# Moving the side work of an encoder layer's MLP rounds to other slots, and four more changes of order

## Chip, cores and metric

The kernel runs on one core of one Trainium2 chip. The metric is the device time of one execution in microseconds (us); lower is better. TensorE is PE here, VectorE DVE, ScalarE ACT, GpSimd POOL, and SP is the engine that issues most DMAs.

## What is computed

One layer of an encoder over 2048 positions of width 1024, all in float32:

```python
u = rmsnorm(h, g_pre_mix)
proj = u @ w_in                                  # q, k, v of group a and of group b
o_a = rmsnorm(windowed_gqa_sink(qa, ka, va, ...), g_out_a)
o_b = rmsnorm(dilated_mixture(qb, kb, vb, ...), g_out_b)   # three dilated patterns, mixed by their weights
h = h + rmsnorm(concat([o_a, o_b]) @ w_o, g_post_mix)
a = relu(rmsnorm(h, g_pre_mlp) @ w_up)           # 4096 wide
h = h + rmsnorm((a * a) @ w_down, g_post_mlp)
gate = sigmoid(h @ w_ple_gate + b_ple_gate)
h = h + rmsnorm(gate * (p @ w_ple_proj), g_post_ple)
```

## The kernel before

Every float32 product is made from three matmuls of a rounded high part and a low remainder (`mm3`: high by high, high by low, low by high). The split of an operand is a pair of operations: ACT copies the value to a rounded high part and DVE subtracts that from the value to give the low part. A matmul has 512 columns as a rule; transposes on PE have 128.

The stages follow one another on PE: input projections; attention of group a; attention of group b; the output projection by tiles of 128 rows (`c_tile`); the MLP; the gate. Up to the end of the MLP the engines' instructions stand in the order that the code issues them. A clock of ticks sets that order: `later(dt, fn)` puts a piece of work `dt` ticks ahead, `tick()` issues what is due. Each engine then works through its own list in order and waits where an operand is not there. Behind the MLP, a scheduler orders the gate stage.

**Group b** has four pairs of heads. `mix` is a generator that joins the three patterns of a pair; each `yield` ends one step, and other work (scores of the next pair, and a filler: `wo_first`, the first part of the output projection, or the ple products `fill2`) is issued between two steps. Its last part turns the weights into a high part `ch` (ACT, L853) and a low part `cl` (DVE, L855), and multiplies both with a selection matrix on PE (`cps`, L861), in 8 parts `rr` of four matmuls; DVE scales the outputs by them (L864) and POOL adds the patterns. The ple products take a buffer for each result (L941, a copy on ACT), which a DMA issued by ACT takes to memory (L942): the first 8 results use the pool `sgt` with 2 buffers, the others 8 slots of `big`. Behind the last pair's scores, a loop issues the last mixer and the filler, and after it `schedule_c` sets the loads (L974), splits (`c_split`, L979 and L980) and norms of the 16 tiles of the output projection.

**`c_tile`** normalises a tile, adds the residual, stores h, normalises again (`norm2`, L1094) and transposes the result by two `turn`s (L1100) into the operands of the MLP. The first products of the MLP's first round (`up`, L173 to L175) are issued beside the last tiles.

**The MLP** has 32 rounds: two halves of the positions by 16 chunks of 256 of its 4096 columns. A round computes its own down products (`down`, L1288) in a two-by-two scheme of seven products, and beside them the up products of the next round. There are 28 ticks, in each three down matmuls and three or four up matmuls: 84 and 96 per round. The last round has no up products. DVE adds the products to `accs` (L1297), but for one product of four parts, ACT copies to `dmp` (L1294) and POOL adds (L1295); POOL also forms the sums of operands (`tmp`, L1132), and DVE their low parts (L1127). Two kinds of foreign work are put in with `later`: a `split_job` prepares a slice of the gate's weight, and a `post_job` (rounds 17 to 24) finishes one tile of the first half's MLP output: load, two squares on ACT (L1207), `rstd` on POOL (L1212 to L1215), two `scale`s (L1219) and two `add`s (L1223) on DVE, a store.

**The gate** has 16 tiles (`d_item`): load of h (`h2`, L1451, three buffers) and of the ple product (`pl`), eight transposes (L146), 48 matmuls (L137 to L139) into `psm`, then the bias (L1474), sigmoid (L1475), product (L1476), norm (L124; L1482), residual (L1483) and the store to `out`. For the first eight tiles it carries along the second half's post work (`post`, L1336 squares, L1345, L1348).

Of the kernel before, what the change touches and what calls it, by code (L numbers as in the profile page):

```python
# [59 lines left out]
def layer(ctx, tc, a, out):  # L60
# [592 lines left out]
    with ExitStack() as st:  # L653
# [159 lines left out]
        def mix(pair, tms, dns):  # L813
# [38 lines left out]
            ch, cl = wr[:, 0], wr[:, 1]  # L852
            act.activation(ch, wt, AF.Copy)  # L853
            yield
            dve.tensor_sub(cl, wt, ch.bitcast(F32))  # L855
            order = range(8) if pair < 3 else (0, 1, 4, 5, 2, 3, 6, 7)
            for n, rr in enumerate(order):
# [14 lines left out]
                if n != 6 or pair == 3:  # L872
                    yield
# [28 lines left out]
        def ple():  # L902
# [26 lines left out]
            for t in range(16):  # L929
                ph_, pl_ = cur  # L930
                for hf in range(2):
# [6 lines left out]
                    if 2 * t + hf == 8:  # L938
                        big = bm.tile([128, 8, 512], F32, name="pst", tag="v1")
                    mx = big[:, (2 * t + hf) % 8] if t >= 4 else sg.tile([128, 512], F32, name="sgt", tag="sgt")  # L940
# [112 lines left out]
    def c_tile(n, t, box):  # L1053
# [3 lines left out]
        cs = [slice(0, 512), slice(512, 1024)]  # L1057

# [33 lines left out]
        def norm2():  # L1092
            box["vn"] = acc_tile(n % 3 if n < 15 else 5)
            dve.scalar_tensor_tensor(box["vn"], box["mx"], box["r2"], gm, op0=ALU.mult, op1=ALU.mult)  # L1094

        def turn(h):
# [4 lines left out]
            if tb < 2:  # L1101
# [9 lines left out]
                4: [norm1], 5: [add], 6: [keep], 7: [norm2], 8: [lambda: turn(0)], 9: [lambda: turn(1)]}, half  # L1111
# [81 lines left out]
    def post_job(t, at):  # L1193
# [179 lines left out]
    with ExitStack() as st:  # L1373
# [5 lines left out]
        stack.append(st.enter_context(ExitStack()))  # L1379
        tp, fd, ap_ = right("tp", 6), right("fd", 4), right("ap_", 3)  # L1380
        fus.append(right("fu2"))
# [12 lines left out]
        jobs = [[(i, k) for i in range(2) for k in range(8)] for _ in range(2)]  # L1394
        for n in range(32):
# [132 lines left out]
```

## Time and profile before

| | us |
|---|---|
| median of 3 runs (2816.85 to 2821.08) | 2817.31 |
| the profiled execution: its own time | 2813.91 |
| the profiled execution: span | 2812.1 |
| PE busy | 2719.5 (97%) |
| DVE busy | 1767.2 (63%) |
| ACT busy | 1273.4 (45%) |
| POOL busy | 931.5 (33%) |

The busy times are of one execution, and the span of its records is 1.8 us shorter than its own time. A matmul's busy time in the profile is modelled, and a busy PE isn't PE at its peak. PEclk is the mean granted clock of TensorE as a share of full speed: 1.00 is 2.4 GHz, 0.50 is 1.2 GHz.

### The profile page before, as it was taken

Reading aid. Unit: us, or ns where it says so; the run is one execution under the profiler, and the core shown is the slowest. Engines: PE = TensorE matmul, PEld = TensorE weight load, DVE = VectorE, ACT = ScalarE, POOL = GpSimd, SP = SyncE. Lnnn points to the kernel's source line nnn. Section 1 sums busy time; section 2 is a strip of 40 time slices with the busy share of each in tenths; the row PEclk is TensorE's granted clock in tenths of the full one; section 3 lists DMA queues with packets and bytes.
Section 4 is the critical chain, followed back from the end, with each engine's and each line's share of the span. In section 5 each row is a group of like instructions: output and inputs, shape, how many; then the busy total and the mean of one; then the engine's idle time right before and its main releaser. Section 6 shows DMA issues by size and latency. Waiting matters only on the chain.

```text
span 2812.1 us, 38924 instructions
## 1 busy us (share of the span) xinstructions
PE 2719.5 (97%) x13952; PEld 2123.9 (76%) x13952; DVE 1767.2 (63%) x3420; ACT 1273.4 (45%) x2940; POOL 931.5 (33%) x950
## 2 busy tenths in 40 slices
PE   7999999999999998999999999999999999999998
PEld 6878866666677676878888888888777778887787
DVE  4210244456666653777778778776788787776665
ACT  4321355566666553555434434445444444443332
POOL 3000033331322301444434434534525344344220
PEclk9999999999999999999999999999999999999999
DMA  5232352325543325872312212234232323224453
GB/s 177 86 116 83 97 157 72 108 78 141 139 93 120 86 97 173 271 237 75 99 63 65 82 60 68 86 134 160 96 106 97 102 90 105 79 72 157 168 192 104
DMA packets 247441, 322.82 MB, mean 115 GB/s; under 512 B 19856, under 2 KB 175504, under 8 KB 244848
## 3 DMA queue, kind: packets, MB, share of 16 engines
q1 hardware_dynamic: 220112, 280.16, 31.6%
q10 hardware_dynamic: 27136, 40.18, 4.0%
q8 instruction: 110, 1.80, 0.3%
q14 instruction: 83, 0.68, 0.1%
HBM read 225.59 MB, written 102.04 MB: 117 GB/s over the span
## 4 chain that ended last, share of the span: by engine, by line
PE 54%; DVE 4%; issue 2%; POOL 1%; ACT 1%; DMA 1%; ACTq 0%; DVEq 0%; POOLq 0%; SPq 0%
PE psd L1288 11%; PE psy L1288 9%; PE psu L174 8%; PE psu L175 8%; PE psu L173 8%; PE psm L137 3%; PE psm L138 3%; PE psm L139 3%; DVE y L1219 1%; PE psd L137 1%; PE psd L139 1%; PE psd L138 1%; DVE acc L1297 1%; POOL acc L1295 1%; DVE y L1223 1%
## 5 line engine op out<-in xcount | busy, mean ns | idle before, releaser
L1297 DVE TENSOR_TENSOR acc<-acc,psd 128x512 f32<-128x512 f32 x488 | 331.3, 685 | 179.5 <-PE psd L1288 174.6
L174 PE MATMUL psu<-vt,uph 128*128 128x512 f32 x1024 | 407.4, 398 | 0.0
L175 PE MATMUL psu<-vt,upl 128*128 128x512 f32 x1024 | 405.0, 395 | 0.0
L173 PE MATMUL psu<-vt,uph 128*128 128x512 f32 x1024 | 402.1, 393 | 0.0
L1132 POOL TENSOR_TENSOR tmp<-rl 128x512 f32<-128x512 f32 x64 | 83.4, 1303 | 691.4 <-ACT rl L1276 691.4
L174 PEld LDWEIGHTS psu<-vt,uph 128*128 128x128 f32 x1024 | 192.3, 188 | 47.9
L173 PEld LDWEIGHTS psu<-vt,uph 128*128 128x128 f32 x1024 | 192.6, 188 | 45.0
L768 ACT ACTIVATE e<-e,tm 128x256 f32<-128x256 f32 (+1 forms) x384 | 176.7, 461 | 107.9 <-DVE tm L765 105.8
L175 PEld LDWEIGHTS psu<-vt,upl 128*128 128x128 f32 x1024 | 192.2, 188 | 43.6
L1297 DVE TENSOR_TENSOR acc<-acc,psy 128x512 f32<-128x512 f32 x248 | 168.8, 684 | 79.2 <-PE psy L1288 72.5
L1275 ACT ACTIVATE rl<-psu 128x512 f32<-128x512 f32 x128 | 76.4, 597 | 305.8 <-PE psu L175 305.8
L1295 POOL TENSOR_TENSOR acc<-acc,dmp 128x512 f32<-128x512 f32 x128 | 192.1, 1512 | 50.5 <-DVE al L1127 31.5
L133 DVE SCALAR_TENSOR_TENSOR wc<-wraw,pre_mix_t,wc 128x128 fp32r<-128x128 f32 x176 | 58.2, 378 | 233.7 <-ACT wc L132 233.7
L1288 PE MATMUL psd<-dnh,al 128*128 128x512 f32 x512 | 203.2, 397 | 0.0
L1288 PE MATMUL psd<-dnh,ah 128*128 128x512 f32 x512 | 201.3, 393 | 0.0
L1288 PE MATMUL psd<-dnl,ah 128*128 128x512 f32 x512 | 201.2, 393 | 0.0
L765 DVE CUSTOM_DVE_ANT_0 e<-ps_s,b 128x256 f32<-128x256 f32 (+1 forms) x384 | 122.7, 375 | 101.9 <-PE ps_s L752 101.6
L173 PE MATMUL psm<-uhi,wc 128*128 128x512 f32 x448 | 181.8, 410 | 0.3 <-ACT uhi L128 0.3
L174 PE MATMUL psm<-ulo,wc 128*128 128x512 f32 x448 | 177.9, 397 | 0.0
L175 PE MATMUL psm<-uhi,wc 128*128 128x512 f32 x448 | 177.6, 396 | 0.0
L1288 PE MATMUL psy<-dnh,ah 128*128 128x512 f32 x384 | 154.2, 402 | 19.0 <-DVE acc L1297 15.0
L1288 PE MATMUL psy<-dnh,al 128*128 128x512 f32 x384 | 153.0, 398 | 0.0
(703 smaller groups left out, 6259.8 us busy)
## 6 DMA issues: line engine op xcount, KB each, us to landing
upraw<-in_w_up_dram SPq DMA_DIRECT2D x64, 512.0 KB, 4.7
dnraw<-in_w_down_dram SPq DMA_DIRECT2D x64, 512.0 KB, 5.2
xt<-in_x_dram SPq DMA_DIRECT2D x32, 512.0 KB, 4.2
h<-hd SPq DMA_DIRECT2D x32, 512.0 KB, 4.4
wraw<-in_w_in_dram SPq DMA_DIRECT2D x26, 512.0 KB, 4.0
qkd<-sgt ACTq DMA_DIRECT2D x52, 256.0 KB, 2.3
mad<-sgt ACTq DMA_DIRECT2D x32, 256.0 KB, 2.0
acc<-mad SPq DMA_DIRECT2D x16, 512.0 KB, 6.3
```

The lines of the kernel that those rows point to most:

```text
L137: pe.matmul(ps, lh(k), rh(k), start=k == 0, stop=False)
L138: pe.matmul(ps, lh(k), rl(k), start=False, stop=False)
L139: pe.matmul(ps, ll(k), rh(k), start=False, stop=k == n - 1)
L173: pe.matmul(ps, lh(k), rh(k), start=k == 0, stop=False)
L174: pe.matmul(ps, lh(k), rl(k), start=False, stop=False)
L175: pe.matmul(ps, ll(k), rh(k), start=False, stop=k == n - 1)
L765: dve.tensor_tensor_reduce(ej, box["ps"][hh][:, 256 * jj : 256 * jj + w], bs[hh] if p == 2 else bs[hh][:, var], scale=1.0, scalar=3.0e38, ...
L768: act.activation(ej, ej, AF.Exp, bias=tm, scale=-1.0, accum_out=box["dn"][p][:, i : i + 1])
L1132: pool.tensor_tensor(t, x, y, op=op)
L1288: pe.matmul(ps, l[:, js], r, start=start and m == 0, stop=m == 2, skip_group_check=True)
L1295: pool.tensor_tensor(t, t, d, op=ALU.add)
L1297: dve.tensor_add(t, t, ps)
```

## The change

Five things are changed, in the order of the code.

1. In `mix`, the high part, the low part and the first `cps` matmuls stand in three steps rather than one and a half, and the 8 parts of the other three pairs are bunched as 0, 1, 2 with 3, 4 with 5, 6 with 7.
2. The ple products use the slots of `big` from their fourth result on, not from the ninth; the loop at the end of group b takes two filler steps always, not three in its first three turns; `schedule_c` is called in its eleventh turn rather than behind it.
3. The two turns of the last two output tiles are issued 3 and 5 ticks later, beside the first round of the MLP, and their results have buffers of their own.
4. In rounds 17 to 24 the steps of `post_job` are spread from ticks 6 to 14 to ticks 8 to 24, and these rounds have no `split_job`; rounds 16 and 25 to 29 have three each.
5. The last round of the MLP gets up's place filled by the gate: the transposes of tiles 0, 1 and 2 and the 96 matmuls of tiles 0 and 1 (`gate_first`), whose h is loaded in round 30. In the gate stage these are left out.

The diff, without the changes to pools and their closing and without repeated arguments:

```diff
@@ mix, the mixer of one pair of heads (group b) @@
             ch, cl = wr[:, 0], wr[:, 1]
+            yield
             act.activation(ch, wt, AF.Copy)
             yield
             dve.tensor_sub(cl, wt, ch.bitcast(F32))
+            yield
             order = range(8) if pair < 3 else (0, 1, 4, 5, 2, 3, 6, 7)
...
-                if n != 6 or pair == 3:
+                if n not in (2, 4, 6) or pair == 3:
                     yield
@@ the ple products, fill2 @@
-                    if 2 * t + hf == 8:
+                    if 2 * t + hf == 3:
                         big = bm.tile([128, 8, 512], F32, name="pst", tag="v1")
-                    mx = big[:, (2 * t + hf) % 8] if t >= 4 else sg.tile([128, 512], F32, name="sgt", tag="sgt")
+                    mx = big[:, (2 * t + hf) % 8] if 2 * t + hf >= 3 else sg.tile([128, 512], F32, name="sgt", tag="sgt")
@@ the end of group b @@
         while mixers:
             advance()
-            for _ in range(3 if loops < 3 else 2):
+            for _ in range(2):
                 next(fill2, None)
+            if loops == 10:
+                schedule_c(4)
+                start = clock[0] + 4
             loops += 1
             tick()
-        schedule_c(4)
-        for _ in range(4):
+        while clock[0] < start:
             next(fill2, None)
             tick()
@@ c_tile, one tile of the output projection @@
+        late = {14: 3, 15: 5}.get(n, 0)
...
-            box["vn"] = acc_tile(n % 3 if n < 15 else 5)
+            box["vn"] = acc_tile(n % 3 if n < 14 else n - 10)
...
-                ... 7: [norm2], 8: [lambda: turn(0)], 9: [lambda: turn(1)]}, half
+                ... 7: [norm2], 8 + late: [lambda: turn(0)], 9 + late: [lambda: turn(1)]}, half
@@ post_job @@
-        for dt, fn in ((0, fetch), (6, lambda: squares(0)), (7, lambda: squares(1)), (8, rstd), (10, lambda: scale(0)),
-                       (11, lambda: scale(1)), (12, lambda: add(0)), (13, lambda: add(1)), (14, keep)):
-            later(at + dt, fn)
+        for dt, fn in ((0, fetch), (8, lambda: squares(0)), (9, lambda: squares(1)), (10, rstd), (15, lambda: scale(0)),
+                       (17, lambda: scale(1)), (20, lambda: add(0)), (23, lambda: add(1)), (24, keep)):
+            later(dt, fn)
@@ before the rounds (new) @@
+        def gate_load():
+            for t in range(3):
+                h = ru.tile([128, D], F32, name="h0", tag="upraw") if t == 2 else vr.tile([128, D], F32, name="h0", tag="vraw")
+                sp.dma_start(h, hd[128 * t : 128 * t + 128, :])
+                heads[t] = [h]
+
+        def gate_turn(t, g):
...
+            ps = psu.tile([128, 4, 128], F32, name="psu", tag="psu")
+            for k in range(4):
+                pe.transpose(ps[:, k, :], h[:, 512 * g + 128 * k : 512 * g + 128 * k + 128], ident)
+            ks = slice(4 * g, 4 * g + 4)
+            act.activation(hi[:, ks], ps, AF.Copy)
+            low = lambda: dve.tensor_sub(lo[:, ks], ps, hi[:, ks].bitcast(F32))
...
+        def gate_first():
+            for hf in range(2):
+                for t in range(2):
+                    _, hi, lo = heads[t]
+                    ps = psu.tile([128, 512], F32, name="psu", tag="psu")
+                    yield from mm3_pieces(ps, 8, ...)
+                    y = heads[t, hf] = ox.tile([128, 512], F32, name="y0", tag="rl")
+                    act.activation(y, ps, AF.Copy)
+                if hf == 0:
+                    gate_turn(2, 0)
+                    gate_turn(2, 1)
@@ the rounds @@
-                for at in ((0, 14) if n < 3 else (0,)):
+                for at in ((0, 10) if n < 3 else (0,)):
                     split_job(0, *jobs[0].pop(0), at)
-            if 17 <= n < 30:
-                if n < 25:
-                    post_job(n - 17, 0)
-                for at in ((16,) if n < 20 else (0, 14) if n >= 25 else (16,)):
-                    if jobs[1]:
-                        split_job(1, *jobs[1].pop(0), at)
+            if 17 <= n < 25:
+                post_job(n - 17)
+            for at in (0, 9, 17) if n == 16 or 25 <= n < 30 else ():
+                if jobs[1]:
+                    split_job(1, *jobs[1].pop(0), at)
...
+            if n == 30:
+                later(20, gate_load)
+            if n == 31:
+                u = gate_first()
             done = 0
             for m in range(28):
                 next(d)
-                while u and done < (m + 1) * 32 // 28:
+                if n == 31 and m < 4:
+                    gate_turn(m // 2, m % 2)
+                while u and done < ((m + 1) * 32 // 28 if n < 31 else (m - 3) * 32 // 24):
                     next(u)
                     done += 1
@@ d_item, one tile of the gate stage @@
             def s2():
+                if t < 3:
+                    box.update(hh=heads[t][1], hl=heads[t][2])
+                    return
...
-                    ps = psm.tile([128, 512], F32, name="psm", tag="psm")
-                    mm3(ps, 8, ...)
+                    if t < 2:
+                        ps = heads[t, hf]
+                    else:
+                        ps = psm.tile([128, 512], F32, name="psm", tag="psm")
+                        mm3(ps, 8, ...)
```

On PE, in the mixer of the first pair, the first `cps` matmuls, the filler (`psm`) and the next pair's scores (`ps_s`, `po`, `pt`) stood so before:

```order
L173 MATMUL psm<-wo,oh__6493 128x512
L174 MATMUL psm<-wo,oh__6493 128x512
L175 MATMUL psm<-wo,ol__6494 128x512
L752 MATMUL ps_s<-bk,bq 128x128 x4
L796 MATMUL po<-et,v_5797 64x128 x4
L779 MATMUL pt<-ident,e 128x128 x4
L861 MATMUL cps<-wr,sel 128x384 x4
L173 MATMUL psm<-wo,oh__6493 128x512
```

and now:

```order
L174 MATMUL psm<-wo,oh__6493 128x512
L175 MATMUL psm<-wo,ol__6494 128x512
L173 MATMUL psm<-wo,oh__6493 128x512
L174 MATMUL psm<-wo,oh__6493 128x512
L175 MATMUL psm<-wo,ol__6494 128x512
L752 MATMUL ps_s<-bk,bq 128x128 x4
L796 MATMUL po<-et,v_5797 64x128 x4
L779 MATMUL pt<-ident,e 128x128 x4
L863 MATMUL cps<-wr,sel 128x384 x4
L752 MATMUL ps_s<-bk,qn 128x256 x4
```

Before, a filler piece with `oh__6493` (six matmuls, of which the row shows the first) still followed the first four `cps`; now all of them stand ahead, and the first `cps` come two steps later, a step being one filler piece and one piece of scores. The line numbers of the changed kernel are 2 to 53 higher.

On DVE, in round 19 (`y` is post_job's tile, `acc` the running sums, `rstd` comes from POOL), the two scales and the first add stood so before:

```order
L1297 TENSOR_TENSOR acc_17773<-acc_17773,psd 128x512
L1127 TENSOR_TENSOR dnl<-tmp,dnh 128x512
L1297 TENSOR_TENSOR acc_17774<-acc_17774,psd 128x512
L1219 SCALAR_TENSOR_TENSOR y_18857<-y_18857,rstd,gb 128x512
L1297 TENSOR_TENSOR acc_17775<-acc_17775,psd 128x512
L1219 SCALAR_TENSOR_TENSOR y_18857<-y_18857,rstd,gb 128x512
L1127 TENSOR_TENSOR al<-tmp,ah 128x512
L1297 TENSOR_TENSOR acc_17776<-acc_17776,psy 128x512
L1223 TENSOR_TENSOR y_18857<-y_18857,h_18859 128x512
L1297 TENSOR_TENSOR acc_17777<-acc_17777,psy 128x512
L1223 TENSOR_TENSOR y_18857<-y_18857,h_18859 128x512
```

and now:

```order
L1302 TENSOR_TENSOR acc_17767<-acc_17767,psy 128x512
L1132 TENSOR_TENSOR al<-tmp,ah 128x512
L1302 TENSOR_TENSOR acc_17768<-acc_17768,psy 128x512
L1224 SCALAR_TENSOR_TENSOR y_18858<-y_18858,rstd,gb 128x512
L1302 TENSOR_TENSOR acc_17773<-acc_17773,psy 128x512
L1302 TENSOR_TENSOR acc_17774<-acc_17774,psy 128x512
L1224 SCALAR_TENSOR_TENSOR y_18858<-y_18858,rstd,gb 128x512
L1302 TENSOR_TENSOR acc_17769<-acc_17769,psy 128x512
L1156 TENSOR_TENSOR upl<-upraw,uph 128x512
L1302 TENSOR_TENSOR acc_17770<-acc_17770,psy 128x512
L1132 TENSOR_TENSOR al<-rl,ah 128x512
L1132 TENSOR_TENSOR dnl<-dnraw,dnh 128x512
```

Both scales now stand behind the adds of the first three parts of `psy`, with other adds between them, and the residual add is further down in another tick.

On SP's queue, the gate stage began so before (`h1` are the tiles of the post work, `h2` those of the gate; `h2_23303` is tile 2 and `h2_23405` tile 3):

```order
L1451 DMA h2_23281<-hd_86 128x1024
L1453 DMA pl_23283<-pled_98 128x1024
L1455 DMA bb_23276<-in_b_ple_gate_dram 128x1024
L1456 DMA gp_23275<-in_g_post_ple_dram 128x1024
L1451 DMA h2_23303<-hd_86 128x1024
L1453 DMA pl_23305<-pled_98 128x1024
L1330 DMA h1_23389<-hd_86 128x1024
L1330 DMA h1_23491<-hd_86 128x1024
L1453 DMA pl_23407<-pled_98 128x1024
L1484 DMA out_0_dram<-y_23323 128x1024
L1451 DMA h2_23405<-hd_86 128x1024
```

and now (`h2_23440` is tile 2, `h2_23476` tile 3, `y_23444` tile 0):

```order
L1500 DMA pl_23432<-pled_98 128x1024
L1498 DMA h2_23434<-hd_86 128x1024
L1500 DMA pl_23436<-pled_98 128x1024
L1498 DMA h2_23440<-hd_86 128x1024
L1500 DMA pl_23442<-pled_98 128x1024
L1335 DMA h1_23460<-hd_86 128x1024
L1335 DMA h1_23496<-hd_86 128x1024
L1500 DMA pl_23478<-pled_98 128x1024
L1500 DMA pl_23514<-pled_98 128x1024
L1537 DMA out_0_dram<-y_23444 128x1024
L1498 DMA h2_23476<-hd_86 128x1024
```

Tile 3's load stands behind the store of tile 0's output in both.

## Rows read from the trace of the kernel before

**Rows 1.** The page of the kernel before: busy us, share of the span, instructions.

```profile
PE 2719.5 (97%) x13952; PEld 2123.9 (76%) x13952; DVE 1767.2 (63%) x3420; ACT 1273.4 (45%) x2940; POOL 931.5 (33%) x950
```

**Rows 2.** Stretches at half clock, by engine; the first row names the columns.

```profile
core 0: us, PE busy (x) PEld busy (x) DVE busy (x) ACT busy (x) POOL busy (x), PEclk, DMA share, GB/s
...
729.85:733.30 3.45, 3.45 (x17) 2.34 (x17) 1.25 (x5) 1.26 (x2) 1.46 (x2) 0.51 0.18 59
...
1067.80:1078.00 10.20, 9.43 (x24) 6.51 (x23) 1.99 (x4) 1.87 (x4) 1.46 (x2) 0.50 0.27 103
1252.10:1255.50 3.40, 3.40 (x14) 2.71 (x11) 2.20 (x4) 2.95 (x6) 1.18 (x3) 0.50 0.53 172
```

**Rows 3.** What PE waited for, 700 to 960 us: us in total, times, longest.

```profile
PE cps L861 <- DVE wr L855: 2.9, 3, 1.0
PE cps L861 <- ACT wr L853: 2.7, 3, 0.9
```

**Rows 4.** What PE waited for, 1040 to 1125 us.

```profile
PE psm L137 <- ACT sgt L941: 7.0, 3, 4.6
PE pss L986 <- POOL o L980: 2.6, 1, 2.6
PE cps L861 <- DVE wr L855: 0.8, 1, 0.8
```

**Rows 5.** What PE waited for, 1236 to 1265 us.

```profile
PE pst L1100 <- DVE acc L1094: 5.1, 2, 4.1
```

**Rows 6.** Timeline of DVE, start of MLP round 0: start us, us, engine, line.

```profile
1260.70 0.68 DVE L1127 TENSOR_TENSOR al<-rl,ah 128x512 fp32r<-128x512 f32 x1
```

**Rows 7.** Engines over a plain round, a round with post work, four gate tiles.

```profile
1868.00:1909.90 41.90, 41.90 (x182) 33.77 (x181) 30.99 (x43) 17.14 (x30) 16.90 (x13) 1.00 0.67 251
...
2000.17:2044.48 44.31, 42.68 (x180) 33.52 (x180) 35.70 (x48) 19.00 (x35) 18.79 (x15) 1.00 0.30 102
...
2617.40:2664.80 47.40, 47.40 (x222) 39.45 (x222) 28.69 (x41) 15.44 (x29) 12.96 (x9) 1.00 0.46 156
```

**Rows 8.** Chain that ended last, end of one post step: start us, us, what.

```profile
2034.29 0.56 POOL rstd L1215
2034.88 1.78 DVE y L1219
...
2038.35 1.71 DVE al L1127
...
2044.48 0.96 PE psy L1288 x3
```

**Rows 9.** DVE by line over round 2000.17 to 2044.48: count, busy us, mean ns.

```profile
L1297 DVE TENSOR_TENSOR acc<-acc,psd 128x512 f32<-128x512 f32 x16 | 11.0, 686 | 6.0 <-PE psd L1288 5.6
```

**Rows 10.** Engines over the last MLP round and over the gate stage.

```profile
2579.90:2607.57 27.67, 21.90 (x85) 16.22 (x84) 22.78 (x32) 8.42 (x15) 12.24 (x8) 0.94 0.59 228
2607.57:2802.60 195.03, 191.16 (x897) 159.12 (x895) 113.85 (x166) 65.83 (x128) 38.71 (x31) 0.98 0.48 165
```

**Rows 11.** Timeline of SP's queue, gate stage.

```profile
2635.08 0.34 SPq L1484 DMA_DIRECT2D out_dram<-y  x1
2635.51 0.38 SPq L1451 DMA_DIRECT2D h<-hd  x1
```

**Rows 12.** Timeline of DVE, gate stage.

```profile
2627.05 0.69 DVE L1474 TENSOR_TENSOR y<-psm,bb 128x512 f32<-128x512 f32 x1 [2.92 <-PE psm L139]
...
2633.84 1.22 DVE L1483 TENSOR_TENSOR y<-y,h 128x1024 f32<-128x1024 f32 x1
```

**Rows 13.** Timeline of ACT, gate stage.

```profile
2609.01 0.61 ACT L1336 ACTIVATE dmp<-acc 128x512 f32<-128x512 f32 x1
...
2619.62 1.28 ACT L1475 ACT_TABLE_LOAD   x1
```

**Rows 14.** Timeline of POOL, gate stage.

```profile
2634.15 3.16 POOL L1348 TENSOR_TENSOR h<-h,acc 128x1024 f32<-128x1024 f32 x1 [2.23 <-DVE acc L1345]
```

**Rows 15.** DMA issues 2600 to 2680 us: count, KB each, us to landing.

```profile
h<-hd SPq DMA_DIRECT2D x11, 512.0 KB, 4.1
```

More of the change, by code (lines that the diff above doesn't have):

```diff
@@ L1110, in c_tile @@
         return {-2: [fetch], 2: [fetch_x, lambda: scaled(1)], 1: [lambda: scaled(0)], 3: [lambda: rms_("r1")],
-                4: [norm1], 5: [add], 6: [keep], 7: [norm2], 8: [lambda: turn(0)], 9: [lambda: turn(1)]}, half
+                4: [norm1], 5: [add], 6: [keep], 7: [norm2], 8 + late: [lambda: turn(0)], 9 + late: [lambda: turn(1)]}, half
     E_ = 32
@@ L1191, in split_job, with post_job @@
             later(at + dt, fn)
-    def post_job(t, at):
+    def post_job(t):
         box = {}
@@ L1379, in layer @@
         stack.append(st.enter_context(ExitStack()))
+        fus.append(right("fu2"))
+        stack.append(st.enter_context(ExitStack()))
         tp, fd, ap_ = right("tp", 6), right("fd", 4), right("ap_", 3)
-        fus.append(right("fu2"))
         while done < 32:
@@ L1394, in layer @@
         jobs = [[(i, k) for i in range(2) for k in range(8)] for _ in range(2)]
+        heads = {}
+        def gate_load():
[4 more added lines that the diff above has]
+        def gate_turn(t, g):
+            pl = fus[t]
+            if g == 0:
+                heads[t] += [pl.tile([128, 8, 128], F32R, name="h" + c, tag="up" + c) for c in "hl"]
+            h, hi, lo = heads[t]
+            ps = psu.tile([128, 4, 128], F32, name="psu", tag="psu")
[5 more added lines that the diff above has]
+            if t < 2:
+                later(1, low)
+            else:
+                low()
+        def gate_first():
[3 more added lines that the diff above has]
+                    ps = psu.tile([128, 512], F32, name="psu", tag="psu")
+                    yield from mm3_pieces(ps, 8, lambda k: hi[:, k, :], lambda k: lo[:, k, :], lambda k: vt[hf][0][:, k, :],
+                                          lambda k: vt[hf][1][:, k, :], 1)
+                    y = heads[t, hf] = ox.tile([128, 512], F32, name="y0", tag="rl")
[3 more added lines that the diff above has]
+                    gate_turn(2, 1)
         for n in range(32):
@@ L1433, in layer @@
         pending = (1, accs)
-        stack[1].close()
+        stack[2].close()
         mlp3.close()
         mlp2.close()
-        keep_.close()
         hp = st.enter_context(tc.tile_pool(name="hp", bufs=2, reuse_waits="tile"))
@@ L1470, in s3 @@
                     cs = slice(512 * hf, 512 * hf + 512)
-                    ps = psm.tile([128, 512], F32, name="psm", tag="psm")
-                    mm3(ps, 8, lambda k: box["hh"][:, k, :], lambda k: box["hl"][:, k, :],
-                        lambda k: vt[hf][0][:, k, :], lambda k: vt[hf][1][:, k, :])
+                    if t < 2:
+                        ps = heads[t, hf]
+                    else:
+                        ps = psm.tile([128, 512], F32, name="psm", tag="psm")
+                        mm3(ps, 8, lambda k: box["hh"][:, k, :], lambda k: box["hl"][:, k, :],
+                            lambda k: vt[hf][0][:, k, :], lambda k: vt[hf][1][:, k, :])
                     dve.tensor_add(y[:, cs], ps, bb[:, cs])
@@ L1499, in layer @@
         run_items([d_item(t) for t in range(16)], lag2=1, lag3=2)
+        stack[1].close()
+        keep_.close()
     mlp1.close()
```

## The prediction

> **What bounds the kernel now.** I read the page first: PE is busy 2719.5 us of 2812.1 [rows 1], so a saving can come only from PE standing still, from PE at half clock, or from PE work taken out. The change takes none out: the matmuls and transposes are the same. So I went through the waits of PE and the granted clock stage by stage, with the chain of waits for the MLP. Five places lose time; each part of the change stands at one of them.
>
> The sum is made against the profiled execution's 2813.9 us. The median of the runs shown is 2817.3, 3.4 above it, and I carry the sum over to that. Less than 0.2%, some 5.6 us, can't be told from no change.
>
> **1. The mixers of three pairs.** In the second half of the attention PE stood three times for the high part of the weights (2.7 us in all) and three times for the low part (2.9 us) [rows 3]: 5.6 us. Each time the clock was then at 1.2 GHz for 3.4 us, and these three stretches look alike; one is shown [rows 2]. At half of 2.4 GHz each costs 1.7 us against the same work at full clock, 5.1 us for three. At most 10.7 us can be won. Now a step of PE work lies between each of the three operations: at least the six matmuls of a filler piece, 1.4 us at the 41.90 / 180 of a plain round [rows 7], more than the about 1 us that each wait took. What could be late next is the eight `cps` now bunched in a step, whose scaling on DVE has fewer fillers beside it; the two parts bunched before (6 and 7) are not among the waits shown, so I cost the bunching at 1 us and a remnant of the waits and the clock at 0.7. I take **-9**; ends -10.7 and -5, where the waits go and the clock stretches stay.
>
> **2. The end of group b.** Over 1040 to 1125 us PE stood 7.0 us for ACT's copy of the ple products, 2.6 for POOL's first sum of the output projection and 0.8 for the last mixer's low part [rows 4], 10.4 us; the clock was at half for 10.2 us behind the first of these [rows 2], worth 5.1. The copies waited for one of two buffers, whose store (a DMA) was under way; eight buffers end that. The split of the first projection tile stood behind all copies on ACT; it now stands ahead of the last ones. At most 15.5 us. What is late next: a load of the attention's output now starts some loops earlier and shares the DMA engines with the ple stores, which ACT issues between its copies, so that an issue that waits holds up the copies behind it; and fewer filler products are left over for the end. I keep back 3.5 for this: **-12**; ends -15.5 and -5.
>
> **3. The last turns of the output projection.** PE stood 5.1 us for `norm2` [rows 5] and ran 3.4 us at half clock behind it [rows 2], 6.8 us in all. The turns now come later and PE goes on with up products. But the MLP's first down products need the low part of their left operand, which DVE makes at 1260.70 [rows 6], behind the same work as before; DVE's order is not changed there. PE gets its up work done sooner and then waits for that operand: what was waited for ahead of it is waited for behind it, except for about a microsecond. And the later turns' results share the two buffers of `sgt` with `dmp`, in the first round of the MLP, where they can hold up PE. I take **-1**; ends -6.8 and +2.
>
> **4. The post jobs.** A plain round takes 41.90 us, one with a post job 44.31 [rows 7]: 2.41 us in each of rounds 17 to 24, 19.3 us. The chain of waits names the cause: `rstd` on POOL behind POOL's adds, `scale` on DVE waiting for it and taking 1.78 us, and behind it on DVE, in order, the low part `al` (1.71 us) and the adds that free the banks of the `psy` products, for which PE waits [rows 8]. Ticks are 1.5 us (41.90 / 28). `rstd` moves by two ticks, the first scale by five, so that three ticks' slack (4.5 us) stand where there was nothing; POOL's order is the same as before, so `rstd` comes no later than the two ticks. DVE's load of such a round is 35.7 us [rows 7], with 6.2 left in a round of 41.90. The split jobs taken out of these rounds go to rounds 16 and 25 to 29, three each; a plain round has 10.9 us of DVE free [rows 7], which covers them, and their loads have five ticks. What may be late next is ACT: the squares stand behind all four `dmp` copies and take their two buffers, so ACT waits for POOL's adds there. I take **-17.5**; ends -19.3 and -9.
>
> The trace shows `scale` and `al`, which read two tensors of SBUF, at 1.7 to 1.8 us, and the adds of `psd`, with one operand in PSUM, at 686 ns on average [rows 8, 9]; at that time POOL was at work. The Trainium skill, in "GPSIMD Engine Reference", section "8. Key points", says that POOL shares its SBUF interfaces with DVE and contends with DVE operations on two SBUF inputs. By that rule the four moved operations stay slow wherever POOL is active, and the move wins only what the wait for `rstd` cost; the trace agrees as to which are slow. The rival below prices it from rows.
>
> **5. The gate's first tiles in the last round.** The last round and the gate took 27.67 + 195.03 = 222.7 us [rows 10]. Now the last round holds the 180 matmuls of a plain round, 41.9 us, and 24 transposes: four gate tiles take 47.4 us [rows 7], 11.85 each, of which 48 matmuls at 41.9 / 180 are 11.2, so eight transposes are some 0.7 to 0.9 and 24 are 2.6. The six turns take the buffers of the up products, freed only when DVE has the low part; I allow 3 us (an estimate: two waits of two or three DVE operations of 0.69). The round ends at 47.5; call that moment E. Without any further wait 14 tiles of matmuls and 13 of transposes would follow (about 165 us), the total would be 212 and the gain above 10.
>
> But PE then holds only tile 2's matmuls, 11 us. Tile 3's load stands on SP behind the store of tile 0, and that store needs all of tile 0's chain. On ACT behind E: a copy, nine squares of the post work at 0.61 each, a table load of 1.28 [rows 13], four sigmoids of a square's length, a norm of twice that width and two DVE operations of 0.69 in between: 12.1. Then `rstd` 0.6 [rows 8] and three passes on DVE, 1.22 each [rows 12]: 16.5. Store and load are issued 0.43 apart [rows 11], and the load takes 4.1 [rows 15]: E + 21. Then tile 3's high parts on ACT stand behind tile 2's sigmoids; these wait for DVE, which stands at tile 1's passes for a `rstd` that POOL does behind a post add of 3.16 [rows 14]: 15.4 + 3.2 + 0.6 + 3.7, two adds, two sigmoids, a copy: E + 26. PE stands from E + 11 to E + 26, but for tile 3's transposes. In the before kernel the chain from the bias add to the store was 8 us long too [rows 11, 12], but PE had two tiles' matmuls in hand. The total is 47.5 + 26.2 + 11 + 12 x 11.85 = 226.9, and 1.7 of half clock behind such an idle, seen behind smaller ones [rows 2]: 5.9 more than before. Since some of the chain may start ahead of E, I take **+5**; ends -13 (no wait) and +10 (two waits).
>
> **Sum.** -9 - 12 - 1 - 17.5 + 5 = -34.5: 2779.4 for an execution like the profiled one, **2783 us** as a median.
>
> **Rivals.**
> - *The gate's start costs nothing.* The loop of tile 3 starts early, since the outputs of tiles 0 and 1 are finished inside the last round and only the post squares delay them. For it: their first halves are copied before E. Against it: the bias and ple tiles are loaded into the space that PE frees last, and the chain above. It would turn +5 into -13, with the turns' waits covered too: 2765. Chance 0.2.
> - *The post jobs still stop PE.* The scales meet POOL's sums, and squares and `dmp` copies dispute two buffers; half of the 19.3 stays: 2792. For it: the DVE operations on two SBUF tensors at 1.7 us [rows 8]; against it: DVE's 6.2 us of slack. Chance 0.14.
> - *The waits of group b only move.* The mixers' chain is as long as before, and a step of PE work may be too short for it; parts 1 and 2 give 6 rather than 21: 2798. Against it: waits of 1 us against steps of 1.4 us and more. Chance 0.1.
> - *Slower.* In the gate the loop of tile t's store, tile t + 3's load and high parts repeats: PE has two tiles, 23.7 us, to cover it; at the start it is 26 long. Were it longer than that for all 12 tiles that follow, by 3.4 us each (a loop of 27.1), it would cost 41 us and undo everything: 2824. From 23.7 us on it costs at all. Against it: the gate before ran 47.40 us without an idle [rows 7]. Chance 0.03.
>
> **The numbers.** The forecast has 0.5, and 0.03 is left for smaller losses. Slower by over 0.2% takes the last rival, 0.03; within 0.2% takes rivals that meet, 0.03; faster 0.94. The range reaches to 2762 (the free gate start) and to 2804 (the third rival, and half of the second on top).
>
> **What would show it.** Rounds 17 to 24 at 41.9 to 42.2 us; no wait of `cps` above 0.3 and full clock at the first three mixers; under 4 us of PE idle from 1040 to 1125; PE idle some 14 us in one stretch after tile 2 of the gate, ended by ACT's copy. I am wrong if that idle is under 5 us (then the time is nearer 2765), if post rounds remain above 43 us, or if half clock remains in group b.

## The result, and the profile after

| | before | changed |
|---|---|---|
| median of 4 runs, us | 2819.11 (2816.85 to 2821.08) | 2802.84 (2799.89 to 2804.38) |
| ratio, 95% interval | | 0.9941 [0.9924, 0.9959] |
| profiled execution, us | 2813.91 | 2803.37 |

The change makes the kernel 0.6% faster, 16.3 us by the medians; the forecast was 34. The profiled execution of before was faster than all four of its runs in the table, so the two traces differ by 10.5 us of span only. The page of the changed kernel, to be read beside [rows 1]:

```profile
span 2801.6 us, 38950 instructions
...
PE 2716.6 (97%) x13952; PEld 2129.1 (76%) x13952; DVE 1755.1 (63%) x3420; ACT 1273.3 (45%) x2944; POOL 933.1 (33%) x950
```

Both traces can be cut at the same matmuls. The start of each on PE (us from the start of the span), and what each piece gained or lost, from that:

| PE reaches | before | changed | piece: changed less before | forecast |
|---|---|---|---|---|
| first scores of group b | 617.23 | 617.99 | +0.8 | |
| last scores of group b | 1031.38 | 1044.38 | **+12.2** (part 1) | -9 |
| first output product | 1120.48 | 1123.41 | **-10.1** (part 2) | -12 |
| last output product | 1236.17 | 1239.09 | 0 | |
| MLP round 1 | 1303.81 | 1309.70 | **+3.0** (part 3) | -1 |
| MLP round 17 | 1974.12 | 1980.01 | 0 | |
| MLP round 31 | 2579.92 | 2566.48 | **-19.3** (part 4) | -17.5 |
| last gate matmul | 2802.56 | 2792.17 | **+3.0** (part 5) | +5 |

By the traces the gain is 10.4 us where 34.5 were forecast. Parts 2, 4 and 5 are within 2 us of their terms, part 3 is 4 us off. The first term has the other sign: 21.2 of the 24 us that are missing.

**Part 1, the mixers.** PE's waits from 700 to 960 us, to be read beside [rows 3]; the columns are us in total, times and longest:

```profile
PE ps_s L752 <- DVE tm L765: 4.9, 2, 2.9
PE pss L612 <- DVE et L782: 4.6, 8, 1.6
PE po L796 <- ACT ops L807: 2.7, 4, 1.0
```

The waits of `cps` for the weights are gone as planned. In their place PE waits for `tm`, which DVE makes from the scores. The timelines at the first mixer tell why. SP's queue (start us, us):

```profile
717.61 7.06 SPq L393 DMA_DIRECT2D v<-vb  x8
724.77 1.11 SPq L599 DMA_DIRECT2D o<-oad  x1
```

ACT, DVE and PE some 7 us later:

```profile
732.04 0.63 ACT L128 ACTIVATE oh__6758<-o 128x512 fp32r<-128x512 f32 x1 [2.67 <-DMA o<-oad]
```

```profile
732.70 0.69 DVE L129 TENSOR_TENSOR ol__6759<-o,oh__6758 128x512 fp32r<-128x512 f32 x1 [4.13 <-ACT oh__6758 L128]
733.31 0.28 DVE L765 CUSTOM_DVE_ANT_0 e<-ps_s,b 128x128 f32<-128x128 f32 x1
```

```profile
728.11 0.72 PE L752 MATMUL ps_s<-bk,bq 64*128 64x128 f32 x8
...
731.32 0.48 PE L752 MATMUL ps_s<-bk,bq 64*128 64x128 f32 x2
733.87 1.22 PE L752 MATMUL ps_s<-bk,bq 64*128 64x128 f32 x6 [2.06 <-DVE tm L765]
```

The load of the filler's next o tile is issued at 724.77, behind eight v loads, and ACT's split of it starts at 732.04, on the load's landing: 7.3 us. DVE's low part stands behind the split, L765 for the scores of 728.11 behind the low part, and PE's next scores behind that: 2.06 us, and 1.04 more at the next `po`. In the before kernel the load took as long (issued at 723.95, split at 731.28), and ACT and DVE waited for it too (DVE's row); PE's scores that stand behind the same split came late there (PE's row):

```profile
731.94 0.69 DVE L129 TENSOR_TENSOR ol__6770<-o,oh__6769 128x512 fp32r<-128x512 f32 x1 [1.85 <-ACT oh__6769 L128]
```

```profile
731.73 1.23 PE L752 MATMUL ps_s<-bk,bq 64*128 64x128 f32 x8
```

PE reached those scores 7.8 us behind the load's issue, after the waits at `cps`, the first `cps` and a filler partly at half clock; in the changed kernel it reaches them after 3.3 us (728.11 less 724.77). The old waits gave the load its time. And the clock: in the changed trace PEclk over 15 us of this mixer and 15 us of the third pair's is as follows (us, busy time of PE, PEld, DVE, ACT, POOL, then PEclk, DMA share, GB/s).

```profile
730.00:735.00 5.00, 2.94 (x15) 2.00 (x13) 2.30 (x12) 2.20 (x7) 0.79 (x2) 0.87 0.20 55
735.00:740.00 5.00, 3.96 (x19) 2.78 (x19) 2.69 (x13) 3.30 (x14) 0.68 (x1) 0.50 0.72 232
740.00:745.00 5.00, 5.00 (x25) 3.40 (x26) 3.15 (x12) 2.51 (x9) 1.45 (x2) 0.61 0.88 322
...
955.00:960.00 5.00, 0.76 (x7) 0.52 (x6) 3.24 (x19) 3.14 (x11) 1.47 (x2) 0.89 0.27 83
960.00:965.00 5.00, 4.81 (x21) 3.71 (x23) 2.22 (x8) 2.36 (x10) 0.40 (x1) 0.50 0.14 52
965.00:970.00 5.00, 5.00 (x24) 3.25 (x20) 3.08 (x12) 2.56 (x9) 1.06 (x2) 0.50 0.00 0
```

Before, some 1.9 us of waits at `cps` per pair were followed by 3.4 us at half clock [rows 2, 3]. Now waits of 3.1 us (first pair) and 4.4 (third) are followed by 10.2 us at half clock (733.7 to 743.9) and 17.1 (958.9 to 976.0). From 700 to 1045 us PE runs 13.6 us at half clock before and 34.1 now, so what PEclk lacks to 1 grows from 6.8 us to 17.0: where PE is busy, that is time lost, and it is most of the 12.2. PE also stands longer: 18.3 us from the second pair's first scores to the last scores, 12.9 before.

**Part 2, the end of group b.** The waits from 1044 to 1125 us, the whole of this piece, beside [rows 4]:

```profile
PE psm L137 <- ACT pst L943: 1.7, 2, 1.1
PE psm L139 <- DVE ol__10374 L129: 1.7, 1, 1.7
PE cps L863 <- DVE wr L856: 0.9, 1, 0.9
```

The 7.0 us for the copies have become 1.7, and the 2.6 us at `pss` and the 10.2 us at half clock [rows 2] are gone.

**Part 3, the last turns.** The waits from 1225 to 1265 us, beside [rows 5]; then DVE and PE at the first down product, beside [rows 6]:

```profile
PE psd L1293 <- ACT ah L1131: 1.9, 1, 1.9
PE pst L1105 <- DVE acc L1099: 1.3, 2, 1.0
```

```profile
1260.28 1.75 DVE L1156 TENSOR_TENSOR upl<-upraw,uph 128x512 fp32r<-128x512 f32 x1
1261.96 1.75 DVE L1132 TENSOR_TENSOR dnl<-dnraw,dnh 128x512 fp32r<-128x512 f32 x1
1263.63 1.75 DVE L1132 TENSOR_TENSOR al<-rl,ah 128x512 fp32r<-128x512 f32 x1
```

```profile
1259.89 0.50 PE L1293 MATMUL psd<-dnh,ah 128*128 128x512 f32 x1 [1.87 <-ACT ah L1131]
...
1265.43 0.79 PE L1293 MATMUL psd<-dnh,al 128*128 128x512 f32 x1 [4.83 <-DVE al L1132]
```

The wait for `norm2` has fallen from 5.1 to 1.3 us, and waits for `ah` (1.87 us) and `al` (4.83 us) have come. `al` starts 24.5 us behind the last output product, as it did before (1260.70 less 1236.17), and takes 1.75 us instead of 0.68: POOL is at its sums then (`tmp`, 1263.13 to 1264.83), and before it was idle from 1260.2 to 1263.4.

**Part 4, the post jobs.** A round with a post job, beside [rows 7], and the scales:

```profile
1979.80:2021.70 41.90, 41.90 (x182) 33.82 (x181) 32.33 (x46) 18.44 (x34) 18.80 (x15) 1.00 0.28 94
```

```profile
L1224 DVE SCALAR_TENSOR_TENSOR y<-y,rstd,gb x16: 744/747/747, 2003.8 to 2299.9; 128x512 f32<-128x512 f32 x16
```

All eight rounds take 41.9 us (335.1 from round 17 to round 25, 354.5 before), and the view of PE's waits from 1990 to 2345 us is empty. The scale takes 747 ns where it took 1.2 to 1.8 us: at its new tick POOL's sums are over. The Trainium skill says in "GPSIMD Engine Reference", section "8. Key points", that POOL shares its SBUF interfaces with DVE and contends with DVE operations on two SBUF inputs; here the trace agrees.

**Part 5, the gate.** The waits of PE from 2540 to 2800 us, and the end of the chain that ends last (start us, us):

```profile
PE pst L146 <- DMA h<-hd: 10.5, 1, 10.5
PE psu L1416 <- DVE hl L1419: 1.3, 1, 1.3
PE psu L173 <- DVE hl L1419: 1.0, 1, 1.0
```

```profile
2624.01 1.05 ACT pl L124 x2
...
2628.45 1.14 DVE y L1536
2629.62 3.93 DMA out_dram<-y
...
2634.73 1.22 DVE y L1536
...
2636.58 1.23 ACT y L1528 x2
...
2638.35 0.79 PE psm L137
```

The last matmuls start at 2613.96 us in the last round and at 2625.19 in tile 2; tile 3's first matmul comes at 2638.35. The forecast put the last two 11 and 26 us behind the round's end; they came 11 and 24.4 behind it, by the chains that were worked out (the norm of tile 0, its store and the load; the sigmoid and copy behind DVE's passes). PE stood 10.5 us in one stretch, not some 14, and the load ended it; ACT's copy held it only 0.3 us more.

### The profile page after: what moved, and what is told of

It is laid out like the page before. It is cut to its first block, busy times and chain, and to the rows that moved or that the text cites. A ratio compares the mean times of both kernels' runs of the same rounds, so it can differ in the third digit from the quotient of the medians.

```text
span 2801.6 us, 38950 instructions
## 1 busy us (share of the span) xinstructions
PE 2716.6 (97%) x13952; PEld 2129.1 (76%) x13952; DVE 1755.1 (63%) x3420; ACT 1273.3 (45%) x2944; POOL 933.1 (33%) x950
## 4 chain that ended last, share of the span: by engine, by line
PE 53%; DVE 1%; ACT 1%; issue 0%; DMA 0%; POOL 0%; DVEq 0%; POOLq 0%; ACTq 0%
PE psd L1293 13%; PE psy L1293 10%; PE psu L174 9%; PE psu L175 9%; PE psu L173 8%; PE psm L137 2%; PE psm L138 2%; PE psm L139 2%; PE pst L146 0%; ACT dmp L1341 0%; ACT y L1528 0%; DMA out_dram<-y 0%; DVE dnl L1132 0%; DVE y L1536 0%; DVE hl L1419 0%
## 5 line engine op out<-in xcount | busy, mean ns | idle before, releaser
L765 DVE CUSTOM_DVE_ANT_0 e<-ps_s,b 128x256 f32<-128x256 f32 (+1 forms) x384 | 122.7, 375 | 105.0 <-PE ps_s L752 104.7
```

Of the source, the lines that this page charges most:

```text
L765: dve.tensor_tensor_reduce(ej, box["ps"][hh][:, 256 * jj : 256 * jj + w], bs[hh] if p == 2 else bs[hh][:, var], scale=1.0, scalar=3.0e38, ...
```

## The experiments

Eleven kernels were run, each beside runs of the kernel before on the same chip. Medians are compared with the changed kernel's 2802.8. It was not run again beside them; the medians of before beside them are 2818.4 to 2820.2 us, so 2 us between two medians say nothing.

**The mixers of pairs 0 to 2 as before.**

```diff
@@ mix @@
-            yield
+            if pair == 3:
+                yield
             act.activation(ch, wt, AF.Copy)
...
-            yield
+            if pair == 3:
+                yield
...
-                if n not in (2, 4, 6) or pair == 3:
+                if n != 6 or pair == 3:
```

> The changed kernel with the mixers of pairs 0 to 2 put back as they were (high part, low part and first cps in one and a half steps, only parts 6 and 7 bunched). In the changed trace the last score matmul of group b comes 12.8 us later than before the change. Theory: the old waits of PE for the mixer's weights gave the load of the filler's next o tile time to land; without them PE comes to the filler's split too early and stands there. Then this kernel has the old waits of about 1 us at cps again, no wait of ps_s behind DVE, the last scores at 1031 to 1032 us, and the time falls by 12 to 13 us, to about 2790. Rival: the 12.8 us come from something else in group b that the change touches (the ple products, the bunched loops at its end); then the last scores stay at 1040 us or later and the time within 3 us of 2803.

Measured: 2795.1 us (ratio to before 0.9913 [0.9899, 0.9928]), 7.7 less (12 to 13 were expected). From the second pair's first scores to the last scores it takes 328.4 us instead of 339.5 (327.0 before). I take this stretch from here on, because the first pair's, ahead of all mixers, differs by itself between the runs (85.7 to 89.1 us among kernels that are alike there). PE's waits, 700 to 1045 us:

```profile
PE cps L865 <- DVE wr L857: 3.0, 3, 1.0
PE cps L865 <- ACT wr L855: 2.7, 3, 0.9
```

So 11 of the 12.5 us that the change lost in this stretch come from part 1, and the old waits return with its undoing. The last scores came at 1036.7 us, not at the 1031 to 1032 of the theory; the first pair took 1.9 us more there and began 2 us later.

**The filler's o load one step earlier.**

```diff
@@ wo_first @@
-                            if hf == 0 and n == 0:
-                                halves, norm = load_o(wop, raws, "wraw", ps_t, "pt", oad, t + 1)
+                            if t == 0 and hf == 0 and n == 0:
+                                after_ = load_o(wop, raws, "wraw", ps_t, "pt", oad, 1)
                             if hf == 1 and n == 0:
+                                halves, norm = after_
                                 nxt = halves()
+                            if t < 14 and hf == 1 and n == 1:
+                                after_ = load_o(wop, raws, "wraw", ps_t, "pt", oad, t + 2)
```

> The changed kernel, with the filler's load of the next o tile issued one step earlier, right behind the split of the tile before it, so that it stands ahead of the eight v loads on SP. Theory (a late o load): the waits of ps_s for DVE (4.9 us) and the long stretches at half clock go, the mixers' old waits don't come back, the last scores come at 1020 to 1025 us, and the time falls by 18 to 23 us, to 2780 to 2785. Rival (the bunched parts of the mixer, or more work on DVE in a step, are what PE waits for): the waits stay, and the time stays within 4 us of 2803.

Measured: 2793.1 us (0.9908 [0.9893, 0.9923]), 9.7 less. The stretch takes 329.1 us instead of 339.5. PE's waits, 700 to 1045 us:

```profile
PE pss L612 <- DVE et L782: 5.9, 11, 1.6
PE po L796 <- ACT ops L807: 4.3, 5, 1.3
PE cps L863 <- DVE ops L866: 2.6, 8, 0.5
```

The wait for `tm` is gone: the late load is shown to be the cause of the loss. But the forecast's 9 us did not come either: the stretch takes no less than the 327.0 of before. That part of the expectation failed. In the trace of before, the first two of these waits are, over the same 345 us:

```profile
PE pss L612 <- DVE et L782: 4.3, 10, 0.4
PE po L796 <- ACT ops L807: 1.6, 3, 0.9
```

and that at `cps` for DVE's scaling is 0.3. The 5.6 us for the weights are gone, and 6.6 us have come at these three places: PE stands 13.8 us in the stretch, 12.9 before. The next run asks what of this the bunches cost.

**The same, without the bunches.**

```diff
@@ mix, beside the edit above @@
-                if n not in (2, 4, 6) or pair == 3:
+                if n != 6 or pair == 3:
```

> The kernel with the earlier o load, with the mixers' parts of pairs 0 to 2 also taken one by one again (only 6 and 7 together). In the run with the earlier load the last scores came at 1032.1 us, no sooner than before the change, though the waits for the mixers' weights were gone; PE waited 2.6 us for DVE's scaling at cps and 5.9 us at pss. Theory: the bunched parts cost that; then the waits at cps fall to 0.3 us and the last scores come 3 to 5 us sooner, at about 1028 us, and the time is 2788 to 2790. Rival: the loss sits in the steps where the weights are split (a wait of 1.6 us at po, with 10 us of half clock behind it, in the mixers of pairs 1 and 2); then the last scores stay within 1.5 us of 1032 and the time at 2792 to 2795.

Measured: 2784.1 us (0.9879 [0.9864, 0.9894]). In this kernel the mixers are two steps longer than the next pair leaves room for, so their last parts mix outputs that the next pair has begun to overwrite, and its results are wrong; PE, DVE, ACT and POOL do the same work. The stretch takes 321.5 us: 7.6 less than with the bunches, and less than with the old mixers (327.0 to 331.2 in the four traces that have them). PE's wait for DVE at `cps` falls from 2.6 us to 0.5:

```profile
PE cps L863 <- DVE ops L866: 0.5, 3, 0.2
```

So splitting the steps without bunches is worth 5 to 10 us, about the 9 forecast, and the bunches, which keep the mixer within its room, give much of it back. (The 1.6 us that the rival puts at `po` stood at `pss`; at `po` the longest wait was 1.3.) How much they cost is not one number: another kernel with the same mixers and the same early load (the last one below) takes 324.9 us, so it is 3.4 by one trace and 7.6 by the other, and 9.0 between the medians of the two runs. The traces show why. PE stands 13.8 us in the stretch in both kernels with bunches and 10.7 without: 3.1 us of standing. But it runs 20.4 us at half clock in the one with bunches, 10.2 in the other, and 6.8 without: the waits in the two with bunches are alike, and the clock behind them is not. The bunches had been costed at 1 us.

**The end of group b as before.**

```diff
-                    if 2 * t + hf == 3:
+                    if 2 * t + hf == 8:
...
-                    mx = big[:, (2 * t + hf) % 8] if 2 * t + hf >= 3 else sg.tile(...)
+                    mx = big[:, (2 * t + hf) % 8] if t >= 4 else sg.tile(...)
...
-            for _ in range(2):
+            for _ in range(3 if loops < 3 else 2):
                 next(fill2, None)
-            if loops == 10:
-                schedule_c(4)
-                start = clock[0] + 4
...
+        schedule_c(4)
```

> The changed kernel with its second part undone (ple results in two buffers up to the ninth, three filler steps in the first turns, the output projection's loads behind the loop). Between the last scores and the first output product the change saved 10.1 us in the traces. Theory: that is part 2's own; this kernel needs 10 us more there (89 us against 79) and the time is 2811 to 2814. Rival: the gain there comes from the mixer of pair 3, whose steps part 1 splits; then at most 4 us are lost, 2803 to 2807.

Measured: 2815.8 us (10 runs, 0.999 [0.998, 1.0001]), 13.0 more, 2 above the range expected. From the last scores to the first output product it takes 89.0 us instead of 79.0. PE stands again for the copies, and longer than before the change at `pss`, for POOL's first sum (1049 to 1140 us):

```profile
PE pss L988 <- POOL o L982: 5.2, 1, 5.2
PE psm L137 <- ACT sgt L943: 3.5, 3, 1.6
```

The rival falls, since pair 3's split steps are still in. The other 3 us are not part 2's by this trace: it has 2.7 us more in the stretch of group b and 1.4 in the output products. What each of part 2's three edits is worth was not tested.

**The post jobs at their old ticks, without split jobs beside them.**

```diff
@@ post_job @@
-        ... (8, squares(0)), (9, squares(1)), (10, rstd), (15, scale(0)), (17, scale(1)), (20, add(0)), (23, add(1)), (24, keep)
+        ... (6, squares(0)), (7, squares(1)), (8, rstd), (10, scale(0)), (11, scale(1)), (12, add(0)), (13, add(1)), (14, keep)
```

> The changed kernel with post_job's steps at their old ticks (6 to 14), but with the split jobs left out of these rounds as in the change. Theory: the scale that waits for rstd is the cause; rounds 17 to 24 take 44.3 us again, and the time is 2820 to 2823. Rival: the split jobs in these rounds were the cause; then the rounds stay at 41.9 us and the time at 2803.

Measured: 2820.0 us (10 runs, 1.0009 [1.0, 1.0018]), 17.2 more; the rounds take 44.3 us, with the wait of before:

```profile
PE psy L1293 <- DVE acc L1302: 12.1, 16, 1.3
```

The ticks are the cause, not the split jobs. Whether the slack for `rstd` or the way out of POOL's sums did more was not tested.

**The last turns at their old ticks.**

```diff
@@ c_tile @@
-        late = {14: 3, 15: 5}.get(n, 0)
+        late = 0
...
-            box["vn"] = acc_tile(n % 3 if n < 14 else n - 10)
+            box["vn"] = acc_tile(n % 3 if n < 15 else 5)
```

> The changed kernel with the last two output tiles' turns at their old ticks. In the changed trace the way from the last output product to the start of MLP round 1 is 3.0 us longer than before. Theory: the idle time only moved to the first down products, whose al is no earlier, and the matmuls that follow it run at half clock with the turns among them; then this kernel's round 1 starts 3 us sooner (about 1306.5 us) and the time is 2799 to 2801. Rival (the forecast's): late turns win about 1 us; then the time is 2804.

Measured: 2801.6 us (0.9938 [0.9921, 0.9954]), 1.3 less, which the runs' spread does not tell from none. The trace does: from the last output product to round 1 it takes 67.4 us instead of 70.6 (67.6 before), with the old wait:

```profile
PE pst L1105 <- DVE acc L1099: 5.2, 3, 3.9
```

**Four buffers for the gate's h.**

```diff
-                h = hp.tile([128, D], F32, name="h2", tag="h2", bufs=3)
+                h = hp.tile([128, D], F32, name="h2", tag="h2", bufs=4)
```

> The changed kernel with four buffers rather than three for the gate's h tiles, so that tile 3's load doesn't wait for tile 0's store; it then stands ahead of that store on SP. In the changed trace PE stands 10.5 us for that load, and tile 3's first matmul comes 24.4 us behind the end of the last MLP round. Theory: two chains end nearly together there, the load and ACT's high part behind tile 2's sigmoids (which wait for DVE behind tile 1's passes); with the load out of the way the other one ends it, and PE's first matmul of tile 3 comes at most 2 us sooner: 2801 to 2803. Rival: the load alone held PE; then 8 to 10 us go: 2793 to 2795.

Measured: 2800.4 us (0.9935 [0.992, 0.995]), 2.4 less. From round 31 to the last gate matmul 221.3 us, against 225.7 (222.6 before): 4.4 less in the trace (the medians alone can't tell). Tile 3's first matmul comes at 2631.06, 17.0 us behind the round's end instead of 24.4, so the theory's 2 us were wrong and the rival's 8 were nearly there; 3.0 of the 7.4 are lost again behind it. PE now waits for:

```profile
PE psm L137 <- ACT hh__23516 L128: 4.4, 1, 4.4
PE psm L139 <- DVE hl__23517 L129: 2.0, 1, 2.0
```

The chain that the theory saw behind the load does not hold PE, because ACT's order is another with the load early (the gate stage is put in order by the scheduler): tile 3's high part now stands ahead of tile 2's sigmoids, right behind the squares of the post work; in the changed trace it stands behind the sigmoids.

```profile
2630.44 1.05 ACT L128 ACTIVATE hh__23516<-pst 128x512 fp32r<-128x512 f32 x2
2639.90 1.23 ACT L1528 ACTIVATE y<-y 128x512 f32<-128x512 f32 x2 [8.41 <-DVE y L1527]
```

**Parts 2 and 4 alone.**

```diff
@@ the kernel before, with the second and fourth part of the change, and with @@
+            if pair == 3:
+                yield
             act.activation(ch, wt, AF.Copy)
             yield
             dve.tensor_sub(cl, wt, ch.bitcast(F32))
+            if pair == 3:
+                yield
```

> The kernel before the change, with its second part (the end of group b, with the split steps of pair 3's mixer) and its fourth (the post jobs) alone. Theory: by the traces these two are all that wins, 10 and 19.3 us, and parts 1, 3 and 5 lose the rest; the time is 2789 to 2792. Rival: parts 3 and 5 are worth something only together with the rest, or part 2 wins only behind the late end that part 1 makes; then the time is 2795 to 2803.

Measured: 2787.2 us (0.9887 [0.9872, 0.9901]): 15.6 less than the whole change, and 31.2 less than before beside it. Two of the five parts, with pair 3's split steps, win all of it; the other three together cost 15.6.

**Versions that keep more.** All three are the changed kernel with the earlier o load, the old ticks of the turns and four buffers of h; they differ in the mixers of pairs 0 to 2:

```diff
@@ mix: the first has it as before the change, the third as in the change, the second so @@
-            yield
+            if pair == 3:
+                yield
             act.activation(ch, wt, AF.Copy)
...
-                if n not in (2, 4, 6) or pair == 3:
+                if n not in (4, 6) or pair == 3:
```

> The changed kernel with the mixers of pairs 0 to 2 and the last turns as before the change, the o load one step earlier, and four buffers for the gate's h: parts 2, 4 and a mended part 5. Theory: as the run with parts 2 and 4 alone (2787.2 us), less 1.4 us, by which the gate with four buffers beats the one of before in the traces (221.3 against 222.6 us from the start of the last round); the earlier load does nothing here, since the old waits for the mixers' weights give it time: 2785 to 2787. Rival: the load was late before the change too; then 3 us more go: 2781 to 2784.

> As the run before it, but the mixers of pairs 0 to 2 get one step more (between the low part and the first cps) and give one back (parts 4 and 5 in one step). Theory: one step more hides both weights, the o load is there, and of the cost of bunching only half is left; against the old mixers 3 to 8 us go: 2778 to 2783. Rival: any step more moves the wait to another place in it (po, pss) and half clock stays; then the time is that of the run before it, within 2 us.

> As the run with old mixers, but with the mixers of the change (three steps, three bunches). Theory: the bunching takes what the split steps give, as in the run with the earlier load alone, where the last scores came as late as before the change: within 3 us of the run with old mixers, 2784 to 2789. Rival: the split steps win with the load in time: 2776 to 2780.

Measured: 2786.5 us (0.9885 [0.9871, 0.99]), 2786.5 (0.9886 [0.9871, 0.9901]) and 2783.6 (0.9877 [0.9861, 0.9894]). The third is the fastest kernel of this study that computes all of the reference: 1.2% below before, 0.7% below the change. Its stretch in group b takes 324.9 us; the kernel with one extra step takes 328.2 and the one with the old mixers 330.1. The old mixers came out as expected. One step did not do what was expected of it: the waits for the weights are gone, but PE stands 2.9 us at `cps` for `tm`, as its rival said. The 2.9 us between the medians are at the limit of what the runs can tell. Well clear of it is that the load in time turns the mixers of the change from a loss of 12 us into none: their stretch takes 339.3 to 342.2 us in the five traces with the late load, 324.9 and 329.1 in the two with the early one.

## Why the prediction was wrong

- **Total.** 2783 forecast, 2802.8 measured: inside the range given, but 16 us of gain instead of 34. The rival "the waits of group b only move" (2798, chance 0.1) is nearest. The waits did move, but not for its reason, a mixers' chain too long for a step, and parts 1 and 2 together cost 2 us instead of giving 6. (Of the range, 2762 is 3 us below the rival that it names, 2765; nothing in the sums says why.)
- **Part 1 is the step that failed.** "Now a step of PE work lies between each of the three operations", and "so I cost the bunching at 1 us": -9, and even the bad end was -5. Measured +12.2. The step hides the weights, as forecast; the waits at `cps` for them are gone. Two things stood against it. The o load, which the sum puts at nothing, takes 7.3 us from issue to its reader, and PE reached the scores behind the filler's split 3.3 us after the issue instead of 7.8; that cost 10 to 15 (339.5 us against 329.1 and 324.9 with the earlier load). And the bunches cost 3 to 9, not 1. "What could be late next" was asked of DVE and the step, not of the DMA queue: before's own trace had DVE waiting for that load (1.85 us) while PE did not. No end of this part's range went above zero, though a wait that moves can cost more than it did.
- **Half clock** was counted as something that can be won back with the waits, never as something to lose: stretches of 3.4 us became 10.2 and 17.1. The prediction's own sign, "if half clock remains in group b", came.
- **Part 2**: right; -10.1 for -12, and confirmed by undoing. PE stood 5.4 us from 1040 to 1125 us, where under 4 were to show it.
- **Part 3**: the mechanism was right (the wait moves to the first `al`), the size not: +3.0 for -1. PE stands 8.0 us at these places instead of 5.5 and runs 6.8 us at half clock instead of 3.4. DVE's order is the same, as the prediction says, but its `al` takes 1.75 us beside POOL's sums, and PE comes to `ah` too early as well.
- **Part 4**: right, -19.3 for -17.5; nothing was late next, and the scales got faster besides.
- **Part 5**: right, +3.0 for +5. The round ended 47.5 us after its start, as forecast, and both chains behind it ended within 2 us of theirs; the rival "the gate's start costs nothing" fell.

## What to carry to other kernels

A wait that is removed gives its time to the next late thing: before you book the gain, look for waits of the other engines, above all for DMA landings, that were hidden behind it in the old trace, and move those loads ahead first. Count half clock behind the new waits as a cost, not only the old stretches as a gain. When steps are split and others bunched to make room, price the bunch with the same care as the split. Work that is moved beside other work helps where the engine waited for a neighbour's result (the post jobs) and not where PE only meets its next operand sooner (the last turns).

## What was not expected of the hardware

- Idle of 2.06 and 1.04 us within 5 us was followed by more than 10 us at 1.2 GHz (PEclk 0.50 from 735 to 740, 0.61 from 740 to 745), where 1.87 us of idle at `cps` before were followed by 3.4 us. The same waits (0.89 and 0.99 us) were followed by 6.8 us in the trace of parts 2 and 4 alone: how long half clock lasts behind like waits is not the same from trace to trace.
- `scale` on two tensors of SBUF takes 0.747 us where POOL is idle, and up to 1.79 us beside POOL's sums, 2.4 times as long.
- The scores of group b's first pair, untouched, take between 85.7 and 89.1 us from trace to trace, for the most part by the clock (PE stands 8.4 and 8.6 us where PEclk is 0.92 and 0.96, and they take 88.5 and 85.7); from 2 to 3 us in one trace of this stage nothing can be concluded.
